# Light experts: float32 weights in two 64-column tiles instead of split weights

## The chip, the cores and the metric

The kernel runs on one core of one Trainium2 chip. The core has five engines that run side by side: TensorE (PE, matrix multiply; its weight loads are listed as PEld), VectorE (DVE), ScalarE (ACT), GpSimd (POOL) and SyncE (SP, which here issues the DMAs). SBUF is the on-chip memory, and PSUM holds what TensorE writes. The metric is the device time of one execution in microseconds (us). Before the change three runs took 1611.48 to 1615.12 us, with a median of 1612.86 us.

## The reference

The program is a trunk of two layers over 256 tokens of width 1024: attention, an output mix, a layer norm, a feed-forward part, a gate and another layer norm. Layer 0 has a dense feed-forward part. Layer 1, which the change touches, has eight experts, of which each token uses two:

```python
gates = jnp.sum(jax.nn.one_hot(top_idx, N_EXPERTS, dtype=jnp.float32) * top_w[..., None], axis=-2)
out = jnp.zeros_like(x)
for e in range(N_EXPERTS):
    out = out + gates[..., e:e + 1].astype(x.dtype) * _swiglu(x, w1[e], w3[e], w2[e])
```

`_swiglu` is `(silu(x @ w1) * (x @ w3)) @ w2`. Of each expert `w1` and `w3` are 1024 x 3584 and `w2` is 3584 x 1024, all float32, so one expert has 44 MB of weights and the eight have 352 MB. Every weight is read once from HBM.

## The kernel before

All matrix products are made in float32r, a format in which TensorE reads a float32 number with reduced precision. To get the precision back, a number is split in two, a rounded `hi` and the rest `lo`: ScalarE casts to `hi` and VectorE subtracts (`Trunk.split`, lines 94 to 96). A product then is three matmuls, hi x hi, hi x lo and lo x hi (`mm3`, lines 251 to 255).

The expert part is the class `Experts` (line 1098 on). Tokens are gathered per expert by a matmul with a one-hot matrix. Experts are ranked by how many tokens chose them. The four that have most, the heavy ones, get 128 token slots each, and the other four, the light ones, 64 each. Tokens that find no slot are served afterwards in a branch that is skipped where there are none.

The weights of an expert are cut along the 3584 hidden columns into blocks of 1024, 1024, 1024 and 512 columns. A block of 1024 is 12 chunks of 1 MB: four of `w1` (kind 0), four of `w3` (kind 1), four of `w2` (kind 2). There are 336 chunks in all, half of them of light experts. The order is fixed when the program is written: two heavy blocks, then light and heavy blocks in turn, with the `w2` chunks of one block laid between the `w1` and `w3` chunks of the next (`parts`, `run`). So a light block's chunks stand beside a heavy block's.

A chunk goes through three places:

- SP issues its DMA into a raw buffer. There are seven, in the order of the list `MOE_RAW` (line 38), and chunk g+7 takes the buffer of chunk g. SP works in order, so a DMA that waits for its buffer holds all later ones.
- ACT and DVE split it into a hi/lo pair of buffers, of which there are four (`MOE_HL`, line 39). After that the raw buffer is free. Splits are written three chunks ahead of the matmuls (`MOE_LEAD`, line 40).
- PE multiplies with the pair. For a heavy expert each 512 columns of one 128-row slice take three matmuls (lines 253 to 255). For a light expert the 64 tokens' hi and lo stand side by side as one 128-column stationary operand: one matmul multiplies both with the weight's hi (line 1232), and a second one the tokens' hi with the weight's lo (line 1233, 64 columns). These are two matmuls in place of three.

A light result thus comes out as two halves in partitions 0 to 63 and 64 to 127, which have to be added. `turn` (line 1278) transposes and adds them at once, by matmuls in plain float32 with the matrix `fold` (line 1288). Then follow Silu on ACT (line 1300) and the product and a new split on DVE (lines 1306 to 1309). A heavy block has Silu and product first and then plain transposes (line 1295). When an expert is done, `close` (line 1336) splits its result, spreads it over the tokens by matmuls (lines 1344 and 1345) and adds it on DVE (line 1349). The last layer norm (lines 651 to 690) ends the program.

Of the kernel before, what the change touches and what calls it, by code (L numbers as in the profile page):

```python
# [19 lines left out]
KT = D // 128  # L20
# [16 lines left out]

MOE_RAW = ["misc", "act", "act", "raw", "raw", "raw", "raw"]
MOE_HL = ["K", "Q", "hl", "hl"]
MOE_LEAD = 3  # L40
HEAVY = 4
# [11 lines left out]
class Trunk:  # L53
# [764 lines left out]
    def route(self, r, N, PL, gate):  # L818
# [60 lines left out]
        r = dict(iota=iota, gate=wt, s1=s1, xs=xs, moe=moe, fold=fold, rank=rank)  # L879
        moe.start(r, PL)  # L880
# [7 lines left out]
        for job in moe.gather(0):  # L888
            job()()
        moe.prepare(4)  # L890
        sums = [lambda tb=tb, j=j: self.ple_sum(PL, [x], t[tb][j], tb, j) for tb in range(2) for j in range(2)]
# [206 lines left out]
class Experts:  # L1098
    def __init__(self, T):
        self.T, self.nc = T, T.nc  # L1100
        self.w = [T.io[n][0] for n in ("moe_w1", "moe_w3", "moe_w2")]
        nb = len(BLOCKS)
        heavy = [(p, b) for p in range(HEAVY) for b in range(nb)]
        light = [(p, b) for p in range(HEAVY, NE) for b in range(nb)]
        self.blocks = [heavy.pop(0), heavy.pop(0)]
        while heavy or light:
            for q in (light, heavy):
                if q:
                    self.blocks.append(q.pop(0))
# [8 lines left out]
        self.raws, self.hl, self.who = [], [], {}  # L1118
        self.jobs, self.pending, self.spread = [], [], {}
        self.hots, self.xe, self.A, self.H, self.Y = {}, {}, {}, {}, {}  # L1120
# [41 lines left out]
    def prepare(self, upto):  # L1162
        T = self.T
        while len(self.hl) < min(upto, len(self.chunks)):
            g = len(self.hl)
            self.fetch(g + 1)
            raw = self.raws[g]
            tag = MOE_HL[g % len(MOE_HL)]
# [21 lines left out]
    def gather(self, g):  # L1190
# [4 lines left out]
        def part(k0):  # L1195
            if k0 == 0:
                self.xe[ps[0]] = T.act([2, KT, CAP], F32R)
                if len(ps) > 1:
                    two = T.act([2, KT, CAP], F32R)
                    for i, p in enumerate(ps[1:]):  # L1200
                        self.xe[p] = two[:, i]
                    self.xe[g, "two"] = two
            hot = self.hots[g]
# [9 lines left out]
            def out():  # L1213
# [3 lines left out]
                if len(ps) > 1:  # L1217
                    two = self.xe[g, "two"]
                    hi, lo = two[:, :, ks, :LIGHT], two[:, :, ks, LIGHT:]
                    src = pt[:, :, CAP:].rearrange("p k (l c) -> p l k c", l=2)  # L1220
                    self.nc.vector.tensor_copy(hi, src)
                    self.nc.vector.tensor_tensor(lo, src, hi.bitcast(F32), op=OP.subtract)

# [3 lines left out]

    def mul(self, out, p, two, hi, lo, first, last):
        mm = self.nc.tensor.matmul
        if not self.light(p):  # L1230
            return self.T.mm3(out, *two, hi, lo, first, last)
        full = lambda: mm(out, two, hi, start=first, stop=last)  # L1232
        half = lambda: mm(out[:LIGHT], two[:, :LIGHT], lo, start=False, stop=False)  # L1233
        for f in (half, full) if last else (full, half):
            f()

    def up(self, i, kind, c, P):
        p, b = self.blocks[i]
        hi, lo = self.hl[self.at[i, kind, c]]
        xe, n = self.xe[p], hi.shape[1]  # L1240
        for k in range(n):
            kk = n * c + k
            two = xe[:, kk, :] if self.light(p) else (xe[:, 0, kk, :], xe[:, 1, kk, :])
            for m, pt in enumerate(P):
                f = slice(512 * m, 512 * (m + 1))
                self.mul(pt, p, two, hi[:, k, f], lo[:, k, f], kk == 0, kk == KT - 1)

    def down(self, i, c):
        p, b = self.blocks[i]
        hi, lo = self.hl[self.at[i, 2, c]]  # L1250
        if b == 0 and c == 0:
            self.Y[p] = [self.T.ps([512], "accB" if self.light(p) else "accA") for _ in range(2)]
        n = self.width(i) // 128
        for k in range(2):
            kk = 2 * c + k
            h = self.H[i][kk // 4]
            two = h[:, kk % 4, :] if self.light(p) else (h[0][:, kk % 4, :], h[1][:, kk % 4, :])
            for m in range(2):
                f = slice(512 * m, 512 * (m + 1))
                self.mul(self.Y[p][m], p, two, hi[:, k, f], lo[:, k, f],  # L1260
                         b == 0 and kk == 0, b == len(BLOCKS) - 1 and kk == n - 1)

    def gated(self, i, kind, P):
        T, nc = self.T, self.nc
        if self.light(self.blocks[i][0]):
            got = [T.s2k([512], tag=("prob", "ckv")[kind]) for _ in P]
            for t, p in zip(got, P):
                nc.scalar.copy(t, p)
            self.A[i, kind] = got
        elif kind == 0:  # L1270
            self.A[i, 0] = [T.s2k([512], tag="prob") for _ in P]
            for t, p in zip(self.A[i, 0], P):
                nc.scalar.activation(t, p, AF.Silu)
        else:
            for t, p in zip(self.A[i, 0], P):
                nc.vector.tensor_tensor(t, t, p, op=OP.mult)

    def turn(self, i):
        T, nc = self.T, self.nc
        self.H[i] = []  # L1280
        todo = []
        cols = lambda t: t.rearrange("m (c p k) -> m c k p", c=2, k=2)
        if self.light(self.blocks[i][0]):
            for a, b in zip(self.A.pop((i, 0)), self.A.pop((i, 1))):
                pt = T.ps([2, 4, LIGHT])
                for n, t in enumerate((a, b)):
                    for k in range(4):
                        nc.tensor.matmul(pt[:, n, k, :], cols(t)[:, k // 2, k % 2, :], self.r["fold"],
                                         start=True, stop=True)
                todo.append((pt, T.shape(a[:, :4 * LIGHT], [4, LIGHT])))  # L1290
        else:
            for s in self.A.pop((i, 0)):
                pt = T.ps([4, 128])
                for k in range(4):
                    nc.tensor.transpose(pt[:, k, :], cols(s)[:, k // 2, k % 2, :], T.ident)
                todo.append((pt, None))

        for pt, s in todo:
            if s is not None:
                nc.scalar.activation(s, pt[:, 0], AF.Silu)  # L1300
        for pt, s in todo:
            if s is None:
                h = T.s2k([4, CAP], F32R, "probT"), T.s2k([4, CAP], F32R, "probT")
                T.split(*h, pt)
            else:
                nc.vector.tensor_tensor(s, s, pt[:, 1], op=OP.mult)
                h = T.s2k([4, CAP], F32R, "probT")
                nc.vector.tensor_copy(h[:, :, :LIGHT], s)
                nc.vector.tensor_tensor(h[:, :, LIGHT:], s, h[:, :, :LIGHT].bitcast(F32), op=OP.subtract)  # L1309
            self.H[i].append(h)  # L1310
# [25 lines left out]
    def close(self, p):  # L1336
        T, r = self.T, self.r
        yy = T.scatter_split(self.Y.pop(p))

        def add(tb, j):  # L1340
            hotT = self.spread[p]["hotT"]
            t = slice(tb * 128, (tb + 1) * 128)
            pt = T.ps([512])
            self.nc.tensor.matmul(pt, hotT[:, t], yy[j][0], start=True, stop=False)
            self.nc.tensor.matmul(pt, hotT[:, t], yy[j][1], start=False, stop=True)

# [28 lines left out]
    def run(self):  # L1375
        T, nc = self.T, self.nc
        n = len(self.blocks)
        for i in range(n + 1):
# [5 lines left out]
            for kind, cs in self.parts(i):  # L1384
                b = i - (kind == 2)
                if kind < 2:
                    P = [T.ps([512]) for _ in range(self.width(i) // 512)]
                for c in cs:
# [164 lines left out]
```

## Time and profile before

| | |
|---|---|
| median of three runs | 1612.86 us |
| the profiled execution, its own time | 1612.92 us |
| its span, first to last instruction | 1611.2 us |
| PE busy | 1559.6 us, 97% of the span |
| PEld busy | 1324.3 us, 82% |
| DVE busy | 1349.8 us, 84% |
| ACT busy | 1093.6 us, 68% |
| HBM read | 467.21 MB |

The profile is of one execution. "Busy" is the time in which at least one instruction of the engine ran. Matmuls overlap each other at their ends, so a matmul's listed duration is longer than the distance from its start to the next one's start. Where this text counts the cost of a stream of matmuls it goes by that distance. A matmul in plain float32 leaves two records in this profile for one instruction of the program (224 instructions of line 1288, 448 records), and one in float32r or a transpose leaves one. The form `128*64 128x512` of a matmul means that 128 rows by 64 columns of weights were loaded and 512 columns were streamed past them. The expert weights arrive between about 641 and 1578 us.

### The profile page before, as it was taken

To read this page: it belongs to the slowest core of one execution; us is meant where nothing else is said; L and a number is where in the kernel's file an instruction comes from. 1 tells how busy PE (TensorE), PEld (TensorE's weight loads), DVE (VectorE), ACT (ScalarE), POOL (GpSimd) and SP (SyncE) were. 2 spreads that over 40 slices of the span, in tenths; PEclk is the share of its full clock that TensorE was granted. 3 is DMA by queue.
4 is the path that set the end of the run, shared out by engine and by line. 5 is a ranking of instruction groups with operands and counts; after the bars stand their busy time and mean duration, and the time that the engine had idled before them with its cause. 6 is when DMAs were issued, how large, how long until landed. Compare 5 with 4: busy or idle time off the path is not lost. (4 is left out here: it accounts for less than half of the span.)

```text
span 1611.2 us, 23371 instructions
## 1 busy us (share of the span) xinstructions
PE 1559.6 (97%) x8969; PEld 1324.3 (82%) x8969; DVE 1349.8 (84%) x1383; ACT 1093.6 (68%) x1185; POOL 66.3 (4%) x113
## 2 busy tenths in 40 slices
PE   8999999999999999989999999999999999999995
PEld 7999989999899999877877876777777777768773
DVE  5797766454668977789999999999999999999997
ACT  4577555444556674667888777768777887787883
POOL 3310000000012001000000000000000000000000
PEclk9999999999999999999999999999999999999998
DMA  8354646555542746669999999999999999999992
GB/s 286 101 167 154 221 161 201 184 188 193 193 144 56 214 162 218 236 224 350 399 407 412 410 407 379 387 355 404 405 389 386 378 394 411 401 379 383 407 407 112
DMA packets 164981, 469.84 MB, mean 292 GB/s; under 512 B 10120, under 2 KB 68560, under 8 KB 150528
## 3 DMA queue, kind: packets, MB, share of 16 engines
q1 hardware_dynamic: 162400, 462.19, 77.1%
q0 software_dynamic: 2176, 5.58, 1.4%
q8 instruction: 72, 1.18, 0.3%
q10 hardware_dynamic: 288, 0.52, 0.1%
q14 instruction: 45, 0.37, 0.1%
HBM read 467.21 MB, written 1.05 MB: 291 GB/s over the span
## 5 line engine op out<-in xcount | busy, mean ns | idle before, releaser
L96 DVE TENSOR_TENSOR hl<-raw,hl 128x1024 fp32r<-128x1024 f32 (+3 forms) x304 | 454.4, 1509 | 129.0 <-ACT hl L95 128.0
L95 ACT CAST hl<-raw 128x1024 fp32r<-128x1024 f32 (+3 forms) x304 | 384.9, 1281 | 200.3 <-PE mm L255 110.7
L255 PE MATMUL mm<-act,hl 128*128 128x256 f32 x1080 | 307.2, 285 | 0.0
L253 PE MATMUL mm<-act,hl 128*128 128x256 f32 x1080 | 307.1, 284 | 0.0
L254 PE MATMUL mm<-act,hl 128*128 128x256 f32 x1080 | 306.5, 284 | 0.0
L253 PEld LDWEIGHTS mm<-act,hl 128*128 128x128 f32 x1080 | 207.9, 192 | 1.3
L254 PEld LDWEIGHTS mm<-act,hl 128*128 128x128 f32 x1080 | 207.7, 192 | 0.8
L255 PEld LDWEIGHTS mm<-act,hl 128*128 128x128 f32 x1080 | 207.7, 192 | 0.4
L96 DVE TENSOR_TENSOR Q<-raw,Q 128x2048 fp32r<-128x2048 f32 (+1 forms) x52 | 114.5, 2205 | 7.6 <-ACT Q L95 7.4
L96 DVE TENSOR_TENSOR K<-raw,K 128x2048 fp32r<-128x2048 f32 (+1 forms) x52 | 114.6, 2205 | 5.4 <-ACT K L95 5.3
L96 DVE TENSOR_TENSOR hl<-act,hl 128x2048 fp32r<-128x2048 f32 x48 | 109.1, 2286 | 2.7 <-ACT hl L95 2.4
L95 ACT CAST Q<-raw 128x2048 fp32r<-128x2048 f32 (+1 forms) x52 | 96.0, 1849 | 20.9 <-PE mm L254 9.6
L1232 PE MATMUL mm<-hl,act 128*128 128x512 f32 x256 | 102.2, 399 | 1.2 <-DVE act L1349 1.2
L95 ACT CAST K<-raw 128x2048 fp32r<-128x2048 f32 (+1 forms) x52 | 95.9, 1847 | 10.9 <-PE mm L254 6.4
L95 ACT CAST hl<-act 128x2048 fp32r<-128x2048 f32 x48 | 91.0, 1914 | 17.4 <-PE mm L254 12.2
L1233 PE MATMUL mm<-hl,act 128*64 128x512 f32 x256 | 98.8, 399 | 0.0
L254 PE MATMUL mm<-hl,act 128*128 128x512 f32 x192 | 75.7, 394 | 2.7 <-DVE hl L96 2.7
L253 PE MATMUL mm<-hl,act 128*128 128x512 f32 x192 | 75.9, 395 | 0.0
L255 PE MATMUL mm<-hl,act 128*128 128x512 f32 x192 | 75.4, 393 | 0.0
L1232 PEld LDWEIGHTS mm<-hl,act 128*128 128x128 f32 x256 | 48.6, 190 | 24.9 <-DVE act L1349 2.6
L1232 PE MATMUL accB<-hl,probT 128*128 128x512 f32 x152 | 60.1, 396 | 2.1 <-DVE probT L1309 2.1
L1233 PE MATMUL accB<-hl,probT 128*64 128x512 f32 x152 | 60.2, 400 | 0.0
(386 smaller groups left out, 3481.0 us busy)
## 6 DMA issues: line engine op xcount, KB each, us to landing
raw<-in_moe_w_dram SPq DMA_DIRECT2D x192, 1024.0 KB, 7.8
act<-in_moe_w_dram SPq DMA_DIRECT2D x96, 1024.0 KB, 10.4
misc<-in_moe_w_dram SPq DMA_DIRECT2D x48, 1024.0 KB, 7.7
raw<-in_w_in_dram SPq DMA_DIRECT2D x35, 1024.0 KB, 5.4
raw<-in_ffn_w_dram SPq DMA_DIRECT2D x33, 1024.0 KB, 5.4
raw<-in_w_out_dram SPq DMA_DIRECT2D x8, 1024.0 KB, 6.0
raw<-in_w_ple_gate_dram SPq DMA_DIRECT2D x8, 1024.0 KB, 5.0
raw<-in_w_uq_dram SPq DMA_DIRECT2D x12, 384.0 KB, 3.3
```

Source lines behind the costliest of these rows:

```text
L95: self.nc.scalar.copy(hi, src)
L96: self.nc.vector.tensor_tensor(lo, src, hi.bitcast(F32), op=OP.subtract)
L253: mm(out, ah, bh, start=first, stop=False)
L254: mm(out, ah, bl, start=False, stop=False)
L255: mm(out, al, bh, start=False, stop=last)
L1232: full = lambda: mm(out, two, hi, start=first, stop=last)
L1233: half = lambda: mm(out[:LIGHT], two[:, :LIGHT], lo, start=False, stop=False)
```

## The change

For the light experts there is no hi/lo split of weights or tokens any more. Their 64 tokens are kept in float32 (`few`), and the raw float32 weights go straight into TensorE as the streamed operand. `side` issues two float32 matmuls with the same 64 token columns: the first takes the left half of the chunk's columns and writes partitions 0 to 63, which is the left 64-column tile of the array, and the second takes the right half and writes partitions 64 to 127, the right tile. One 512-column PSUM tile then holds 1024 result columns, without anything to add up. So `fold` goes, the light blocks take the heavy ones' path of Silu, product and transposes, and `turn` ends in a plain copy. In `close` the two halves are read from the two groups of partitions. A raw buffer of a light chunk is now held until PE is done with it, and a new method `refill` issues further loads after each chunk's matmuls. There are nine raw buffers (two more, from the tag `Q`) and three hi/lo pairs. Splits are written two chunks ahead instead of three. Heavy experts compute as before.

```diff
-MOE_RAW = ["misc", "act", "act", "raw", "raw", "raw", "raw"]
-MOE_HL = ["K", "Q", "hl", "hl"]
-MOE_LEAD = 3
+MOE_RAW = ["misc", "act", "act", "raw", "raw", "raw", "raw", "Q", "Q"]
+MOE_HL = ["K", "hl", "hl"]
+MOE_LEAD = 2
...
-        fold = one([CAP // 2], "fold")
-        nc.vector.tensor_tensor(fold, self.ident[:, :LIGHT], self.ident[:, LIGHT:], op=OP.add)
...
     def prepare(self, upto):
         T = self.T
-        while len(self.hl) < min(upto, len(self.chunks)):
-            g = len(self.hl)
+        while len(self.hl) < len(self.heavy) and self.heavy[len(self.hl)] < upto:
+            g = self.heavy[len(self.hl)]
             self.fetch(g + 1)
             raw = self.raws[g]
...
             T.split(*hl, raw)
-            self.hl.append(hl)
-            self.fetch(g + 1 + len(MOE_RAW))
+            self.hl[g] = hl
+
+    def refill(self, g):
+        while g < len(self.chunks) and (g in self.hl or g in self.used):
+            g += 1
+        self.fetch(g + len(MOE_RAW))
...
-    def mul(self, out, p, two, hi, lo, first, last):
-        mm = self.nc.tensor.matmul
-        if not self.light(p):
-            return self.T.mm3(out, *two, hi, lo, first, last)
-        full = lambda: mm(out, two, hi, start=first, stop=last)
-        half = lambda: mm(out[:LIGHT], two[:, :LIGHT], lo, start=False, stop=False)
-        for f in (half, full) if last else (full, half):
-            f()
+    def side(self, out, lhsT, raw, first, last):
+        n = raw.shape[-1] // 2
+        for m in range(2):
+            self.nc.tensor.matmul(out[m * LIGHT:(m + 1) * LIGHT, :n], lhsT, raw[:, m * n:(m + 1) * n],
+                                  start=first, stop=last)
...
         for k in range(n):
             kk = n * c + k
-            two = xe[:, kk, :] if self.light(p) else (xe[:, 0, kk, :], xe[:, 1, kk, :])
+            if self.light(p):
+                self.side(P[0], xe[:, kk, :], self.raws[g][:, k, :], kk == 0, kk == KT - 1)
+                continue
...
     def turn(self, i):
...
-            for a, b in zip(self.A.pop((i, 0)), self.A.pop((i, 1))):
-                pt = T.ps([2, 4, LIGHT])
-                for n, t in enumerate((a, b)):
-                    for k in range(4):
-                        nc.tensor.matmul(pt[:, n, k, :], cols(t)[:, k // 2, k % 2, :], self.r["fold"],
-                                         start=True, stop=True)
...
+            for k in range(n):
+                nc.tensor.transpose(pt[:, k, :], s[:, k // 2, k % 2, :], T.ident)
+            todo.append((pt, n))
+        for pt, n in todo:
+            if light:
+                h = T.s2k([n, 128], tag="probT")
+                nc.scalar.copy(h, pt)
...
     def close(self, p):
         T, r = self.T, self.r
-        yy = T.scatter_split(self.Y.pop(p))
+        yy = []
+        for y in self.Y.pop(p):
+            yy.append((T.s2k([512], F32R), T.s2k([512], F32R)))
+            T.split(*yy[-1], y)
...
                     else:
                         self.down(b, c)
+                    self.refill(self.at[b, kind, c])
```

What stands in PE's row for the first chunk of the first light block (`act_7748` and `act_7744` are its tokens, `K` the split weights before). Before the change:

```order
L1232 MATMUL mm_7973<-K_7917,act_7748 128x512
L1233 MATMUL mm_7973<-K_7918,act_7748 64x512
L1232 MATMUL mm_7974<-K_7917,act_7748 128x512
L1233 MATMUL mm_7974<-K_7918,act_7748 64x512
L1232 MATMUL mm_7973<-K_7917,act_7748 128x512
L1233 MATMUL mm_7973<-K_7918,act_7748 64x512
L1232 MATMUL mm_7974<-K_7917,act_7748 128x512
L1233 MATMUL mm_7974<-K_7918,act_7748 64x512
L1295 MATMUL mm_7989<-ident,prob_7813 128x128 x4
L1295 MATMUL mm_7994<-ident,prob_7814 128x128 x4
```

And after it, with the three light chunks that follow:

```order
L1230 MATMUL mm_7953<-act_7705,act_7744 64x512 x4
L1289 MATMUL mm_7960<-ident,prob_7807 128x128 x4
L1289 MATMUL mm_7965<-ident,prob_7808 128x128 x4
L1230 MATMUL mm_7953<-raw_7741,act_7744 64x512 x4
L1230 MATMUL mm_7953<-raw_7770,act_7744 64x512 x4
L1230 MATMUL mm_7953<-raw_7802,act_7744 64x512 x4
```

Eight float32r matmuls into two PSUM tiles have become four float32 matmuls into one, left and right tile in turn, and their weights are the raw buffers.

SP's row in the middle of the expert part, with what each DMA waits for. Before:

```order
L169 DMA raw_8577<-in_moe_w_dram 128x2048 [waits DMAHW1_49,DVE_49]
L169 ISA
L169 DMA misc_8591<-in_moe_w_dram 128x2048 [waits DMAHW2_49,DVE_49]
L169 ISA
L169 DMA act_8605<-in_moe_w_dram 128x2x1024
L169 ISA
L169 DMA act_8627<-in_moe_w_dram 128x2x1024 [waits DMAHW3_49,DVE_49]
```

After, at the same place of the queue:

```order
L169 DMA Q_8394<-in_moe_w_dram 128x2048 [waits DMAHW0_49,PE_49]
L169 ISA
L169 DMA misc_8396<-in_moe_w_dram 128x2048 [waits DMAHW1_49,DVE_49]
L169 ISA
L169 DMA act_8398<-in_moe_w_dram 128x2x1024 [waits DMAHW2_49]
L169 ISA
L169 DMA act_8416<-in_moe_w_dram 128x2x1024 [waits DMAHW3_49,DVE_49]
```

Loads that waited for a split on DVE wait for PE now where the buffer's last chunk was a light one, and the buffers `Q` have joined the ring.

## Rows read from the trace of the kernel before

**Rows 1.** Stretches of the run: from:to, length, then the busy time and instruction count of PE, PEld, DVE, ACT and POOL, the granted TensorE clock as a share of full speed, the DMA engines' busy share and the GB/s that they moved. In order: the first expert loads, the body of the expert part, the end of the program, a long dense stretch, and a short one of those with most traffic.

```profile
641.00:735.00 94.00, 87.52 (x433) 71.88 (x432) 78.32 (x131) 58.54 (x74) 1.57 (x2) 0.98 0.68 245
735.00:1578.00 843.00, 823.18 (x3855) 641.55 (x3854) 804.20 (x536) 667.74 (x480) 0.00 (x0) 1.00 1.00 394
...
1578.00:1612.00 34.00, 16.40 (x67) 10.92 (x65) 22.53 (x32) 7.22 (x15) 1.53 (x2) 0.80 0.12 46
...
790.00:900.00 110.00, 108.74 (x508) 83.88 (x507) 105.71 (x68) 91.55 (x66) 0.00 (x0) 1.00 1.02 410
...
1460.00:1470.00 10.00, 10.00 (x59) 8.84 (x59) 8.54 (x9) 5.78 (x5) 0.00 (x0) 1.00 1.03 418
```

**Rows 2.** Who waited for whom from 735 to 1578 us, first of the DMA queue of SP, then of all engines: total us, times, longest us.

```profile
SPq L169 <- DVE hl L96: 291.4, 113, 9.3
SPq L169 <- DVE K L96: 152.2, 53, 9.0
SPq L169 <- DVE Q L96: 148.1, 61, 6.7
...
ACT Q L95 <- PE mm L254: 21.8, 29, 1.4
ACT hl L95 <- PE mm L254: 21.2, 29, 1.5
```

**Rows 3.** Groups of ACT from 735 to 1578 us: the split of one chunk into the pair `K`, with busy us, mean ns and the idle time before them with its causes; the only one of the long groups with a wait for a load.

```profile
L95 ACT CAST K<-raw 128x2048 fp32r<-128x2048 f32 x46 | 88.0, 1913 | 10.0 <-PE mm L254 5.6 <-PE accA L254 2.5 <-DMA raw<-in_moe_w_dram 1.2
```

**Rows 4.** The matmuls of line 1232 over the whole run, by form: count, busy us, mean ns. Line 1233 has the same counts.

```profile
L1232 PE MATMUL mm<-hl,act 128*128 128x512 f32 x256 | 102.2, 399 | 1.2 <-DVE act L1349 1.2
...
L1232 PE MATMUL accB<-hl,probT 128*128 128x512 f32 x152 | 60.1, 396 | 2.1 <-DVE probT L1309 2.1
...
L1232 PE MATMUL mm<-Q,act 128*128 128x512 f32 x96 | 38.7, 403 | 0.0
L1232 PE MATMUL mm<-K,act 128*128 128x512 f32 x96 | 37.6, 391 | 0.0
...
L1232 PE MATMUL accB<-K,probT 128*128 128x512 f32 x36 | 14.2, 393 | 0.9 <-DVE probT L1309 0.9
L1232 PE MATMUL accB<-Q,probT 128*128 128x512 f32 x36 | 14.1, 391 | 0.0
```

**Rows 5.** PE in order of time: start us, us, what. First a piece of a light block, from the first to the ninth of a run of alternating matmuls, then the same of a heavy block.

```profile
1204.99 0.39 PE L1232 MATMUL mm<-Q,act 128*128 128x512 f32 x1
1205.22 0.40 PE L1233 MATMUL mm<-Q,act 128*64 128x512 f32 x1
...
1206.84 0.39 PE L1232 MATMUL mm<-hl,act 128*128 128x512 f32 x1
...
1211.30 0.39 PE L253 MATMUL accA<-K,probT 128*128 128x512 f32 x1
...
1213.12 0.39 PE L255 MATMUL accA<-K,probT 128*128 128x512 f32 x1
```

**Rows 6.** PE in order of time, plain float32: 16 records of 128 columns in the first layer's norm (line 1477) and what follows them, then the 32 fold records of a light block (line 1288), of 64 columns, and what follows.

```profile
221.34 1.95 PE L1477 MATMUL mm<-s2k,act 128*128 128x128 f32 x16
223.04 0.48 PE L253 MATMUL mm<-K,s2k 128*128 128x512 f32 x1
...
1235.13 1.04 PE L1288 MATMUL mm<-fold,prob 128*128 128x64 f32 x8
...
1238.80 0.48 PE L253 MATMUL mm<-Q,act 128*128 128x512 f32 x1
```

**Rows 7.** The fold matmuls over the whole run, by form, and eight transposes of a heavy block in order of time with the matmul after them.

```profile
L1288 PE MATMUL mm<-fold,ckv 128*128 128x64 f32 x224 | 31.0, 281 | 0.0
...
L1288 PE MATMUL mm<-fold,prob 128*128 128x64 f32 x224 | 29.9, 277 | 0.0
...
1203.34 1.34 PE L1295 MATMUL mm<-ident,prob 128*128 128x128 f32 x8 [1.02 <-DVE prob L1276]
1204.44 0.48 PE L1232 MATMUL mm<-Q,act 128*128 128x512 f32 x1
```

**Rows 8.** The largest group of DVE from 735 to 1578 us, one chunk's subtraction each.

```profile
L96 DVE TENSOR_TENSOR hl<-raw,hl 128x2048 fp32r<-128x2048 f32 x90 | 203.6, 2286 | 7.1 <-ACT hl L95 7.1
```

**Rows 9.** Loads of expert weights over the whole run: count, KB each, median us from issue to landing.

```profile
raw<-in_moe_w_dram SPq DMA_DIRECT2D x192, 1024.0 KB, 7.8
act<-in_moe_w_dram SPq DMA_DIRECT2D x96, 1024.0 KB, 10.4
misc<-in_moe_w_dram SPq DMA_DIRECT2D x48, 1024.0 KB, 7.7
```

**Rows 10.** The end of the program in order of time: SP's last issue of expert weights, the split of the last expert's result and its adds on DVE, and the first instruction of the last norm.

```profile
1559.58 6.94 SPq L169 DMA_DIRECT2D raw<-in_moe_w_dram  x4
...
1594.38 1.28 DVE L96 TENSOR_TENSOR s2k<-accB,s2k 128x512 fp32r<-128x512 f32 x2
1595.58 3.38 DVE L1349 SCALAR_TENSOR_TENSOR act<-mm,gate_at,act 128x512 f32<-128x512 f32 x5
1599.10 1.29 DVE L672 BATCH_NORM_STATS2 tiny<-act 128x6 f32<-128x512 f32 x2
```

More of the change, by code (lines that the diff above doesn't have):

```diff
@@ L1117, in __init__ @@
                     self.chunks.append((i - (kind == 2), kind, c))
-        self.raws, self.hl, self.who = [], [], {}
-        self.jobs, self.pending, self.spread = [], [], {}
+        self.raws, self.hl, self.who = [], {}, {}
+        self.heavy = [g for g, (i, kind, c) in enumerate(self.chunks) if not self.light(self.blocks[i][0])]
+        self.jobs, self.pending, self.spread, self.used = [], [], {}, set()
         self.hots, self.xe, self.A, self.H, self.Y = {}, {}, {}, {}, {}
@@ L1197, in part @@
                 self.xe[ps[0]] = T.act([2, KT, CAP], F32R)
[L1198 to L1202, printed above, removed]
+                if g == 1:
+                    self.few = T.act([NE - HEAVY, KT, LIGHT])
+                    for p in range(HEAVY, NE):
+                        self.xe[p] = self.few[:, p - HEAVY]
             hot = self.hots[g]
@@ L1217, in out @@
                 if len(ps) > 1:
[L1218 to L1222, printed above, removed]
+                    self.nc.vector.tensor_copy(self.few[:, ps[1] - HEAVY:ps[2] - HEAVY + 1, ks, :],
+                                               pt[:, :, CAP:].rearrange("p k (l c) -> p l k c", l=2))
@@ L1244, in up @@
             for m, pt in enumerate(P):
                 f = slice(512 * m, 512 * (m + 1))
-                self.mul(pt, p, two, hi[:, k, f], lo[:, k, f], kk == 0, kk == KT - 1)
+                self.T.mm3(pt, xe[:, 0, kk, :], xe[:, 1, kk, :], hi[:, k, f], lo[:, k, f], kk == 0, kk == KT - 1)
+        self.used.add(g)
     def down(self, i, c):
         p, b = self.blocks[i]
-        hi, lo = self.hl[self.at[i, 2, c]]
+        g = self.at[i, 2, c]
         if b == 0 and c == 0:
-            self.Y[p] = [self.T.ps([512], "accB" if self.light(p) else "accA") for _ in range(2)]
+            self.Y[p] = [self.T.ps([512], "accB")] if self.light(p) else [self.T.ps([512], "accA") for _ in range(2)]
@@ L1255, in down @@
             kk = 2 * c + k
+            first, last = b == 0 and kk == 0, b == len(BLOCKS) - 1 and kk == n - 1
+            if self.light(p):
+                h = self.H[i][0]
+                m, at = divmod(kk, n // 2)
+                self.side(self.Y[p][0], h[:, at, m * LIGHT:(m + 1) * LIGHT], self.raws[g][:, k, :], first, last)
+                continue
+            hi, lo = self.hl[g]
             h = self.H[i][kk // 4]
-            two = h[:, kk % 4, :] if self.light(p) else (h[0][:, kk % 4, :], h[1][:, kk % 4, :])
             for m in range(2):
                 f = slice(512 * m, 512 * (m + 1))
-                self.mul(self.Y[p][m], p, two, hi[:, k, f], lo[:, k, f],
-                         b == 0 and kk == 0, b == len(BLOCKS) - 1 and kk == n - 1)
+                self.T.mm3(self.Y[p][m], h[0][:, kk % 4, :], h[1][:, kk % 4, :], hi[:, k, f], lo[:, k, f], first, last)
+        self.used.add(g)
     def gated(self, i, kind, P):
         T, nc = self.T, self.nc
[L1265 to L1272, printed above, removed]
+        if kind == 0:
+            self.A[i] = [T.s2k([p.shape[-1]], tag="prob") for p in P]
+            for t, p in zip(self.A[i], P):
                 nc.scalar.activation(t, p, AF.Silu)
         else:
-            for t, p in zip(self.A[i, 0], P):
+            for t, p in zip(self.A[i], P):
                 nc.vector.tensor_tensor(t, t, p, op=OP.mult)
@@ L1343, in add @@
             pt = T.ps([512])
-            self.nc.tensor.matmul(pt, hotT[:, t], yy[j][0], start=True, stop=False)
-            self.nc.tensor.matmul(pt, hotT[:, t], yy[j][1], start=False, stop=True)
+            rows = slice(LIGHT * j, LIGHT * (j + 1)) if light else slice(0, CAP)
+            for n, y in enumerate(yy[0 if light else j]):
+                self.nc.tensor.matmul(pt, hotT[rows, t], y[rows], start=(n == 0), stop=(n == 1))
             def out():
@@ L1386, in run @@
                 if kind < 2:
-                    P = [T.ps([512]) for _ in range(self.width(i) // 512)]
+                    w = self.width(i)
+                    P = [T.ps([w // 2])] if self.light(self.blocks[i][0]) else [T.ps([512]) for _ in range(w // 512)]
                 for c in cs:
```

39 lines of the change are left out of this document (14 added, 25 removed).

## The prediction

> **What bounds the kernel now.** I read the stretches of the expert part first, because the whole-run shares mix it with layers that the change doesn't touch. From 735 to 1578 us [rows 1] PE is busy 823.18 of 843 us, DVE 804.20 of 843, and the DMA engines show a share of 1.00 at 394 GB/s. Three resources stand near their limit at once, so the question is which one the others wait for. The waits answer it [rows 2]: SP's load queue waited 291.4 + 152.2 + 148.1 = 592 us for splits to give up a raw buffer, and ACT's splits waited for PE to give up a hi/lo pair. Hardly anything waited for a load: one group of ACT shows 1.2 us of it [rows 3]. Weights are there before they are needed, PE eats them up, and everything else is held back by PE. But the reserve behind it is thin: where the loads ran densest for long they moved 410 GB/s (790 to 900 us), and 418 in one of the best 10 us [rows 1], against 394 on average. So a PE that gets much faster runs into the loads after about 4%.
>
> **The light matmuls.** Before, lines 1232 and 1233 ran 256 + 152 + 96 + 96 + 36 + 36 = 672 times each [rows 4], 1344 records of 512 columns. In a light block eight of them start within 1206.84 - 1204.99 = 1.85 us, one each 0.231 us, and in a heavy block within 1213.12 - 1211.30 = 1.82 us, one each 0.2275 us [rows 5]. Light matmuls so cost 1344 x 0.231 = 311 us. Now 608 float32 matmuls of 512 columns and 128 of 256 take their place, as much as 672 of 512. A float32 matmul is two records, so 1344 records of 512 columns again. What remains open is how long one takes, and whether the left and the right tile run at the same time.
>
> The trace has no float32 matmul of 512 columns. The two ends: 0.2275 us, if it streams like the float32r rows; and 0.425 us, if the 128-column float32 records, 16 in 223.04 - 221.34 = 1.70 us, one each 0.106 us [rows 6], are four times as long at four times the columns. They could also be held by their weight loads, since the 64-column fold records are no shorter, 32 in 3.67 us or 0.115 us each [rows 6]; that is why both ends stay open. I take 0.425 us, from the row that is float32 itself. The Trainium skill ("FP8 and Floating Point Precision", TensorE Precision Notes) counts four passes through the array for true float32; with two records that makes two passes each, the upper end, and the sum by it is the same 0.425 us.
>
> No row of before has two column tiles at work at once. Here too there are two ends: one after the other, 1344 x 0.425 = 571 us, or fully side by side, half of it, 286 us. I take side by side: the two matmuls share no array column and no result partition, and each reads its own half of the chunk. That makes 286 - 311 = -25 us. The other corners are 571 - 311 = +260 us (0.425, in turn), 306 - 311 = -5 us (0.2275, in turn) and 153 - 311 = -158 us (0.2275, side by side).
>
> Changing between the whole array and a half of it costs little in this trace: line 1232 loads 128 columns and line 1233 only 64, they alternate, and the step is 0.231 us against 0.2275 us without alternation [rows 5]. The program now goes between light matmuls and others 150 times. I go by the row and count 150 x 0.004 = 0.6 us as nothing. The Trainium skill ("TensorEngine Tiling (Array Packing)", Key Properties) says that a change of the tiling mode drains TensorE, which speaks against such a program. By that rule each change would cost the part of a matmul that the next one overlaps, 0.39 - 0.23 = 0.16 us [rows 5], together 24 us, which the loads' limit below would cover; the 1344 matmuls that alternate here show no such cost.
>
> **Folds, transposes, splits.** The 224 + 224 fold records [rows 7] at 0.115 us go: -51 us. For them 56 plain transposes come (four for a 1024 block, two for a 512 block, for four experts), at (1204.44 - 1203.34) / 8 = 0.1375 us [rows 7]: +8 us. Half of the 336 chunk splits go, 168 x 2.286 = 384 us of DVE [rows 8] and 168 x 1.913 = 321 us of ACT [rows 3]. All of that lies beside PE, so in the sum it counts nothing; it takes DVE from 95% of the stretch to about half. Where a heavy block's transposes wait for DVE now, 1.02 us once [rows 7], a light block has the same wait in place of the fold's chain of ACT and DVE; I count these even. PE's sum is -25 - 51 + 8 = -68 us.
>
> **What is late next.** PE can give back 68 us only if the weights come 68 us sooner. In 843 us at 394 GB/s 332 MB were moved. At 410 GB/s they take 810 us, 33 us less; at 418, 795 us, 48 us less; without any gain in rate, 0. I take 410, the rate of a long stretch. So the loads are late, not PE, and 33 of the 68 us come out. Before 735 us nothing is won: the first 24 chunks are heavy, and PE eats one in 12 x 0.2275 = 2.73 us. Two more raw buffers let 2 MB more be asked for there, between 0 and 5 us at 410 GB/s; I take 0.
>
> At the end PE now follows the loads instead of trailing them. Loads end at about 1578 us (the last is issued at 1566 [rows 10]) and the last norm starts at 1599.10 us, 21 us later. What must stand there: the last chunk's 1.7 us, the split of one result tile instead of two, 0.6 + 0.7 us, and four adds of 0.7 us with their matmuls, together about 7 us. So 0 to 14 us can go; I take half, 7.
>
> **The new waits.** A light matmul waits for its load itself, and the load into a buffer that held a light chunk waits for PE. Behind that waiting load stand all later loads, since SP works in order. Chunk g+9 is asked for when PE is done with g, or two or more chunks sooner after a heavy g. A chunk every 2.56 us (1.05 MB at 410 GB/s) makes nine chunks 23 us, against 7.8 to 10.4 us from issue to landing [rows 9]. So I charge nothing. A heavy split takes 1.9 + 2.3 = 4.2 us, and two light chunks ahead of it last only 3.4 us, but ACT and DVE are free to start when the load lands, and a fixed delay moves all chunks alike; it costs nothing while the loads set the pace.
>
> **Sum.** The profiled execution took 1612.92 us, within 0.1 us of the median, so it needs no correction. 1612.9 - 33 - 7 = 1573 us.
>
> **Rivals.**
>
> 1. The tiles run one after the other. The matmuls are issued in one order on one engine, and nothing in the trace shows two at once. Then PE has +260 - 51 + 8 = +217 us, and as it bounds already, the time is 1830 us. It decides from the gain s of the pairing: PE has 571 / s - 311 - 43, which is a loss below s = 1.61. Against it stands only that the two tiles need nothing of each other.
> 2. They overlap in part, because each float32 matmul is two records that must follow each other in its tile, and the second tile's first record queues behind them. With s from 1.45 to 1.75 PE has +40 to -28 us, and the time is 1585 to 1653 us; in the middle, at 1.60, 357 - 354 = +3 us and 1616 us, no faster than before. The Trainium skill ("TensorE: Matmul & The Clock Gate", Part 3, Measured speedup vs the span model) has 2.38 times for three column tiles, 79% of three; two tiles at 79% would give that 1.59, so 1618 us. No row here shows it.
> 3. The loads don't get faster: they run at 394 GB/s because the DMA engines are as full as they get (a share of 1.00 on average), and buffers held longer eat up the rest. Then only the end gains, 1606 us. For it: the share; against it: 410 GB/s over 110 us.
> 4. A float32 record streams at 0.2275 us. PE gains 48 or 201 us and the loads still bound, so this gives the forecast's 1573 us and is counted with it.
>
> **How the numbers follow.** The forecast with rival 4 gets 0.70; its own range is 1550 us (418 GB/s and all 14 us of the end) to 1600 us (a pairing of 1.8, with small losses between loads and PE). Rival 1 gets 0.13, rival 2 0.12, rival 3 0.05. The range of 1550 to 1640 us takes in the forecast's, rival 3 and most of rival 2, and leaves out rival 1 and what lies beyond the ends, about 0.2. What can be told from no change is 0.2%, about 3 us. Faster is the forecast, 0.70, with rival 3's larger part and a piece of rival 2, 0.75 together; the same is 0.04; slower is rival 1 and most of rival 2, 0.21.
>
> **What would show it.** Right: in a light block the start of the right tile's record lies inside the left tile's, and a chunk's four float32 matmuls (eight records) take about 1.7 us; the DMA rate from 780 us on stands near 410 GB/s throughout; PE shows idle time before light matmuls, released by loads; DVE falls to about half. Wrong: eight records take 3.4 us and PE is busy throughout (rival 1), or 2.1 us and more (rival 2); SP still waits long, now for PE, while the rate stays under 400 GB/s (rival 3). A light record of about 0.23 us would show the upper end of its price wrong without touching the time.

## The result and the profile after

The changed kernel takes 1573.39 us (median of four, 1571.93 to 1575.25) against 1612.34 us of the kernel before. The ratio is 0.9756, with a 95% interval of 0.9739 to 0.9773. The forecast was 1573 us.

The stretches after, in the columns of [rows 1]. The body of the expert part ends earlier now, so it is taken to 1545 us, and the last two rows cover the end of the loads:

```profile
641.00:735.00 94.00, 88.90 (x448) 72.78 (x447) 77.64 (x130) 58.81 (x75) 1.57 (x2) 1.00 0.73 267
735.00:1545.00 810.00, 788.14 (x3601) 486.20 (x3602) 425.97 (x294) 340.89 (x261) 0.00 (x0) 0.99 1.02 406
735.00:780.00 45.00, 45.00 (x206) 29.53 (x206) 27.25 (x19) 21.12 (x16) 0.00 (x0) 1.00 0.89 335
780.00:900.00 120.00, 115.66 (x507) 68.54 (x505) 58.29 (x36) 50.50 (x40) 0.00 (x0) 0.99 1.02 410
900.00:1000.00 100.00, 100.00 (x473) 66.81 (x472) 63.78 (x43) 46.55 (x34) 0.00 (x0) 1.00 1.02 411
...
1530.00:1540.00 10.00, 10.00 (x71) 5.32 (x71) 1.77 (x4) 2.14 (x4) 0.00 (x0) 1.00 1.04 409
1540.00:1550.00 10.00, 9.46 (x53) 3.84 (x50) 1.17 (x2) 0.74 (x2) 0.00 (x0) 1.00 0.72 294
```

From 780 us on the loads move 410 or 411 GB/s in stretch after stretch, where they moved 394 on average before. DVE is busy 426 of 810 us, about half. The loads run dry at about 1547 us (294 GB/s over the last 10 us, against 409 in the 10 before). In the kernel before, 373 GB/s from 1570 to 1580 us put that end at 1579 us by the same reckoning, 32 us later. Of before, in the same columns, the first stretch after 735 us and the two at the end of the loads:

```profile
735.00:780.00 45.00, 45.00 (x210) 35.75 (x209) 43.02 (x31) 36.61 (x26) 0.00 (x0) 1.00 0.95 359
1560.00:1570.00 10.00, 9.87 (x59) 7.98 (x57) 9.96 (x8) 7.98 (x9) 0.00 (x0) 1.00 1.03 401
1570.00:1580.00 10.00, 9.23 (x40) 6.36 (x41) 9.90 (x11) 9.84 (x8) 0.00 (x0) 1.00 0.91 373
```

The last norm (line 672) now starts 12 us behind the loads, where it was 20 us behind them [rows 10]:

```profile
1559.50 1.29 DVE L672 BATCH_NORM_STATS2 tiny<-act 128x6 f32<-128x512 f32 x2 [1.76 <-DVEq L1013]
```

PE's matmuls at the border of a heavy and a light piece: start us, us, what. Then the weight loads of the same light matmuls:

```profile
806.71 0.39 PE L255 MATMUL mm<-hl,act 128*128 128x512 f32 x1
807.03 1.94 PE L1230 MATMUL accB<-raw,probT 128*64 128x512 f32 x8
808.79 1.89 PE L1230 MATMUL accB<-Q,probT 128*64 128x512 f32 x8
```

```profile
807.94 0.14 PEld L1230 LDWEIGHTS accB<-raw,probT 128*64 128x64 f32 x2 [0.28 <-issue]
808.37 0.14 PEld L1230 LDWEIGHTS accB<-Q,probT 128*64 128x64 f32 x2 [0.28 <-issue]
808.80 0.14 PEld L1230 LDWEIGHTS accB<-Q,probT 128*64 128x64 f32 x2 [0.29 <-issue]
```

A chunk's eight records start within 808.79 - 807.03 = 1.76 us, 0.22 us each. By itself that fits two stories: records of 0.43 us side by side, or records of 0.22 us in turn, as in [rows 5]. The weight loads speak for the first: they come two at a time (x2 in one merged row of 0.14 us, the length of a single one), and the next two 0.43 us later. So two records start together and stream for 0.43 us; the one-tile kernel below tests this.

The waits after, from 735 to 1545 us, in the form of [rows 2]: first those of SP, then two of all engines, and last the loads' time from issue to landing, as in [rows 9]:

```profile
SPq L169 <- PE mm L1230: 148.1, 69, 8.6
SPq L169 <- PE accB L1230: 134.2, 39, 6.4
SPq L169 <- DVE hl L96: 70.5, 39, 5.8
```

```profile
ACT hl L95 <- DMA raw<-in_moe_w_dram: 77.8, 27, 10.3
...
ACT hl L95 <- DMA act<-in_moe_w_dram: 46.5, 12, 10.3
```

```profile
raw<-in_moe_w_dram SPq DMA_DIRECT2D x148, 1024.0 KB, 15.9
```

Before, ACT waited for PE and hardly ever for a load. Now it waits for loads, and a load needs 15.9 us from issue to landing instead of 7.8. By an estimate from these figures, 15.9 us at 406 GB/s make 6.5 MB, some six chunks on their way at once, where 7.8 us at 394 GB/s made three. SP's waits for PE are still long, but they cost nothing while the rate stays at 411 GB/s.

### The profile page after: what moved, and what is told of

Read it like the earlier page. It is cut to its first block, busy times and chain, and to the rows that moved or that the text cites. A ratio compares the mean times of both kernels' runs of the same rounds, so it can differ in the third digit from the quotient of the medians.

```text
span 1571.6 us, 22033 instructions
## 1 busy us (share of the span) xinstructions
PE 1519.3 (97%) x8705; PEld 1162.5 (74%) x8705; DVE 961.8 (61%) x1134; ACT 763.4 (49%) x961; POOL 66.3 (4%) x113
## 5 line engine op out<-in xcount | busy, mean ns | idle before, releaser
L96 DVE TENSOR_TENSOR hl<-raw,hl 128x1024 fp32r<-128x1024 f32 (+3 forms) x264 | 365.4, 1392 | 213.4 <-ACT hl L95 205.2
L95 ACT CAST hl<-raw 128x1024 fp32r<-128x1024 f32 (+3 forms) x264 | 309.8, 1183 | 274.7 <-PE mm L255 111.2
L254 PE MATMUL accA<-hl,probT 128*128 128x512 f32 x172 | 72.3, 420 | 16.6 <-DVE hl L96 16.5
L1230 PE MATMUL mm<-raw,act 128*64 128x512 f32 (+1 forms) x440 | 87.1, 537 | 0.0
L253 PE MATMUL accA<-hl,probT 128*128 128x512 f32 x172 | 73.3, 426 | 4.7 <-ACT hl L95 4.7
L96 DVE TENSOR_TENSOR hl<-act,hl 128x2048 fp32r<-128x2048 f32 x22 | 50.3, 2291 | 43.8 <-ACT hl L95 43.8
L255 PE MATMUL accA<-hl,probT 128*128 128x512 f32 x172 | 70.5, 410 | 0.0
L95 ACT CAST hl<-act 128x2048 fp32r<-128x2048 f32 x22 | 42.0, 1907 | 57.4 <-DMA act<-in_moe_w_dram 46.5
L254 PE MATMUL mm<-K,act 128*128 128x512 f32 x172 | 67.4, 392 | 0.7 <-DVE K L96 0.7
L253 PE MATMUL mm<-K,act 128*128 128x512 f32 x172 | 67.5, 392 | 0.0
L255 PE MATMUL mm<-K,act 128*128 128x512 f32 x172 | 67.2, 391 | 0.0
L95 ACT CAST probT<-mm 128x512 fp32r<-128x512 f32 x28 | 15.2, 588 | 106.0 <-PE mm L1289 106.0
L253 PEld LDWEIGHTS mm<-hl,act 128*128 128x128 f32 x276 | 52.0, 188 | 18.9 <-issue 4.9
## 6 DMA issues: line engine op xcount, KB each, us to landing
raw<-in_moe_w_dram SPq DMA_DIRECT2D x148, 1024.0 KB, 15.9
```

Source lines behind the costliest of these rows:

```text
L95: self.nc.scalar.copy(hi, src)
L253: mm(out, ah, bh, start=first, stop=False)
L254: mm(out, ah, bl, start=False, stop=False)
L255: mm(out, al, bh, start=False, stop=last)
L1230: self.nc.tensor.matmul(out[m * LIGHT:(m + 1) * LIGHT, :n], lhsT, raw[:, m * n:(m + 1) * n], start=first, stop=last)
```

## The experiments

**Is it the pairing, and what does it hang on?** Two kernels leave bytes, instructions and records as they are. The first only sorts a light chunk's matmuls (shown for `up`; `down` has the same edit, and `side` gets the tile `t` as an argument):

```diff
-        for k in range(n):
+        for t, k in [(t, k) for t in range(2 if self.light(p) else 1) for k in range(n)]:
...
```

> Only the order of a light chunk's matmuls changes: all of the left tile first, then all of the right tile; the work and the result are the same. Theory (a float32 record of 512 columns takes 0.43 us, matmuls start in order, a tile takes one at a time, and the two tiles run side by side): a tile's four records now follow each other, and only the last of one tile lies beside the first of the other, so a chunk takes 6 steps of 0.43 us instead of 4. 152 chunks x 0.86 us and 16 chunks of the 512 blocks x 1.29 us are +152 us of PE, less the 35 us that PE had to spare: 1690 us, eight records in 2.58 us instead of 1.72. Rival (a record takes 0.22 us and they run one after the other, nothing is side by side): no change, 1573 us. Rival (PE looks past the order): no change either.

Measured: 1574.4 us, ratio 0.9755 (0.9735 to 0.9774), no change. Its weight loads from 807.4 us on:

```profile
807.99 0.15 PEld L1229 LDWEIGHTS accB<-raw,probT 128*64 128x64 f32 x2 [0.28 <-issue]
808.42 0.15 PEld L1229 LDWEIGHTS accB<-raw,probT 128*64 128x64 f32 x2 [0.28 <-issue]
```

They still come in twos every 0.43 us. In a chunk of a 1024 block the right tile's first record now stands four records behind the left tile's first, and the two tiles fill all the same. So the theory's in-order part is wrong there. The time alone doesn't say that the order never matters, since PE has some 37 us to spare (worked out below). In a `w1` or `w3` chunk of a 512 block eight records of 256 columns go to one tile and then eight to the other, and there the order does cost something. Sixteen such records, first in the changed kernel and then in this one:

```profile
915.68 1.90 PE L1230 MATMUL mm<-raw,act 128*64 128x256 f32 x16
915.78 2.81 PE L1229 MATMUL mm<-raw,act 128*64 128x256 f32 x16
```

The 0.91 us more are about four steps of the 0.22 us that such a record takes alone in the next kernel. This fits a right tile that starts four records ahead of its place and no more: behind four left records nothing is lost, and behind eight the first four of the left and the last four of the right run alone. What takes the records out of the program's order, PE itself or a step before it, these runs don't show.

The second kernel puts nearly all matmuls into the left tile. The right half of the result is left out so, and its products are added to the left half:

```diff
         for m in range(2):
-            self.nc.tensor.matmul(out[m * LIGHT:(m + 1) * LIGHT, :n], lhsT, raw[:, m * n:(m + 1) * n],
-                                  start=first, stop=last)
+            t = m if first else 0
+            self.nc.tensor.matmul(out[t * LIGHT:(t + 1) * LIGHT, :n], lhsT, raw[:, m * n:(m + 1) * n],
+                                  start=first, stop=(last and m == 1) or t == 1)
```

> The second of each two light matmuls goes to the left tile too, apart from the first of each sum, which still writes both; the right half of the result is left out and added to the left half. Records, bytes and instructions are as many as before. Theory (side by side): 304 of 336 pairs lose their overlap, 0.86 us each: +261 us of PE, less 35 us to spare: 1799 us, eight records in 3.4 us. Rival (records of 0.22 us one after the other): no change, 1573 us.

Measured: 1798.57 us, ratio 1.1144 (1.1119 to 1.1168). Its matmuls and weight loads in one light piece:

```profile
820.12 3.65 PE L1231 MATMUL accB<-raw,probT 128*64 128x512 f32 x8
823.60 0.59 PE L1231 MATMUL accB<-Q,probT 128*64 128x512 f32 x1
```

```profile
820.60 0.14 PEld L1231 LDWEIGHTS accB<-raw,probT 128*64 128x64 f32 x1 [0.29 <-issue]
821.03 0.14 PEld L1231 LDWEIGHTS accB<-raw,probT 128*64 128x64 f32 x1 [0.29 <-issue]
```

Eight records start within 823.60 - 820.12 = 3.48 us, twice as long, and the weight loads come singly every 0.43 us. Records that stream in less time, with a fixed cost for two in a row in one tile, would look the same at 512 columns. The records of 256 columns rule that out. The busy time of both forms over the whole run of this kernel:

```profile
L1231 PE MATMUL mm<-raw,act 128*64 128x512 f32 x312 | 132.9, 596 | 0.0
...
L1231 PE MATMUL mm<-raw,act 128*64 128x256 f32 x128 | 28.8, 383 | 0.0
```

132.9 / 312 = 0.426 us and 28.8 / 128 = 0.225 us for one: about half for half of the columns. A float32 record of 512 columns so takes 0.43 us, and without the second tile the change would have cost about 185 us.

**Who sets the pace now?** One kernel takes work from PE, one takes bytes from the loads, and one has both edits:

```diff
+        w = n if first or last else n // 2
         for m in range(2):
-            self.nc.tensor.matmul(out[m * LIGHT:(m + 1) * LIGHT, :n], lhsT, raw[:, m * n:(m + 1) * n],
+            self.nc.tensor.matmul(out[m * LIGHT:(m + 1) * LIGHT, :w], lhsT, raw[:, m * n:m * n + w],
```

> Light matmuls other than the first and the last of each sum stream only half of their columns; the other half of these products is left out. Loads are as before. PE loses 272 x 0.43 = 117 us. Theory (the loads set the pace): 1570 to 1573 us, and the rate stays at 411 GB/s. Rival (PE still sets it): 1456 to 1500 us.

```diff
+            if self.light(self.blocks[i][0]) and kind < 2:
+                src, dims = src[:, :dims[0] // 2, :], [dims[0] // 2, dims[1]]
...
```

> Of each light w1 and w3 chunk only the first half is loaded, and it is multiplied twice; the other half of these weights is left out. PE's work is as before, and the loads are 112 x 0.52 = 59 MB fewer, 143 us at 411 GB/s. Theory (the loads set the pace, with PE 35 us behind): PE sets it now, 1530 to 1550 us. Rival (something else than the loads sets the pace): 1573 us. Rival (loads alone, PE far from the limit): 1430 us.

> Both cuts together: half of the light w1 and w3 weights is not loaded (the other half is multiplied in its place), and light matmuls stream half of their columns but for the first and the last of each sum. Theory (two limits, loads first and PE 35 us behind): PE has 117 us less and the loads 143 us less, so 1430 to 1460 us, well under either cut alone. Rival (a third limit, as the heavy splits or the chain of Silu, product and transposes): about the 1530 to 1550 us of the loads' cut alone.

Measured: 1570.04 us with less for PE (ratio 0.9725, 0.9709 to 0.9742), 1536.78 us with fewer loads (0.9522, 0.9506 to 0.9538), 1445.87 us with both (0.896, 0.8934 to 0.8987). The dense stretch of the changed kernel, then of the first of these, in the columns of [rows 1]:

```profile
780.00:1545.00 765.00, 743.14 (x3397) 456.68 (x3397) 398.72 (x275) 319.77 (x246) 0.00 (x0) 0.99 1.02 410
780.00:1545.00 765.00, 670.89 (x3391) 468.72 (x3389) 395.39 (x274) 316.79 (x244) 0.00 (x0) 0.93 1.02 410
```

And of the second:

```profile
780.00:1510.00 730.00, 730.00 (x3399) 450.27 (x3398) 395.23 (x275) 317.39 (x245) 0.00 (x0) 1.00 0.93 356
```

With less work PE stands idle for 94 of 765 us, the loads stay at 410 GB/s, and the time hardly moves. Its busy time falls by 72 us and not by the 117 us of the expectation, because the granted clock averages 0.93 of full speed there instead of 0.99: at full speed it would be 743.14 x 0.99 - 670.89 x 0.93 = 112 us, an estimate. With fewer loads PE is busy all the time, and the rate falls to 356 GB/s. So the loads set the pace of the changed kernel, with PE close behind: 1573.39 - 1536.78 = 37 us. With both cuts the time falls as far as the theory of two limits has it, so no third one stands near them.

**The buffers.** First seven raw buffers,

```diff
-MOE_RAW = ["misc", "act", "act", "raw", "raw", "raw", "raw", "Q", "Q"]
+MOE_RAW = ["misc", "act", "act", "raw", "raw", "raw", "raw"]
```

> Seven raw buffers instead of nine, all else as in the changed kernel. Theory (nine buffers are more than the loads need): seven chunks of 2.56 us are 18 us, against 8 to 10 us from issue to landing without a queue, so 1573 to 1580 us. Rival (a buffer held until PE is done needs the depth): 1590 us or more, with the load rate under 400 GB/s.

and then also the pairs and the distance of before:

```diff
-MOE_HL = ["K", "hl", "hl"]
-MOE_LEAD = 2
+MOE_HL = ["K", "Q", "hl", "hl"]
+MOE_LEAD = 3
```

> Seven raw buffers, four hi/lo pairs and splits three chunks ahead, as before the change, with the new light matmuls. Theory (the gain is the matmuls', not the buffers'): 1573 to 1580 us, as with seven buffers alone. Rival (the buffers bring the gain): 1590 us or more.

Measured: 1577.36 us, ratio 0.9766 (0.9745 to 0.9786), and 1580.93 us, ratio 0.9797 (0.9771 to 0.9823). The first can't be told from the changed kernel's 0.9756, the second lies some 0.4% above it. So two raw buffers fewer cost at most a few us, though PE holds those of light chunks longer now.

**Was freeing DVE and ACT worth nothing?** The prediction had said so. This kernel splits the light chunks again, and nothing reads their pairs:

```diff
...
-        while len(self.hl) < len(self.heavy) and self.heavy[len(self.hl)] < upto:
-            g = self.heavy[len(self.hl)]
+        while self.split_to < min(upto, len(self.chunks)):
+            g = self.split_to
+            self.split_to += 1
...
             T.split(*hl, raw)
-            self.hl[g] = hl
+            if not self.light(self.blocks[self.chunks[g][0]][0]):
+                self.hl[g] = hl
```

> ACT and DVE split the light chunks too, into the three pairs in turn, and nobody uses the result; the light matmuls read the raw buffers as in the changed kernel. That puts 168 x 2.29 = 384 us of DVE and 322 us of ACT back. Theory (splits lie beside the work that sets the pace): DVE has 783 us to do in a body of 810 us, so 1573 to 1590 us. Rival (freeing DVE is what made the kernel faster): back to 1605 us or more.

Measured: 1609.77 us, ratio 0.9982 (0.9972 to 0.9992). The rival's time came: nearly all of the gain is gone. Whether its reason holds, DVE alone, is tested below. The stretch from 735 to 1545 us, and PE's two longest waits from 735 to 1578 us:

```profile
735.00:1545.00 810.00, 769.14 (x3461) 474.87 (x3459) 751.04 (x443) 617.13 (x409) 0.00 (x0) 0.99 1.00 393
```

```profile
PE accA L254 <- DVE K L96: 21.4, 13, 4.1
PE accA L254 <- DVE hl L96: 16.3, 11, 2.4
```

The loads are back at 393 GB/s, and PE waits 38 us for heavy splits. ACT in turn waits for PE to release a pair. From 735 to 1545 us the two longest of these waits, which with two shorter ones make 150 us, are

```profile
ACT K L95 <- PE accA L254: 49.8, 21, 4.9
ACT hl L95 <- PE mm L254: 44.1, 54, 1.8
```

Three more kernels put the idle splits into the pair `Q` of their own, with seven raw buffers: both halves of a split, DVE's half alone and ACT's half alone. In the kernel with both halves the added lines are

```diff
+            if self.light(self.blocks[self.chunks[g][0]][0]):
+                self.fetch(g + 1)
+                raw = self.raws[g]
+                hi, lo = [T.act(list(raw.shape[1:]), F32R, tag="Q") for _ in range(2)]
+                T.split(hi, lo, raw)
+                continue
```

and the other two have `T.nc.vector.tensor_tensor(lo, raw, raw, op=OP.subtract)` or `T.nc.scalar.copy(hi, raw)` in the place of `T.split(hi, lo, raw)`.

> The idle splits of light chunks again, but into a pair of their own (the buffers Q), so that the heavy chunks keep their three pairs for themselves; seven raw buffers, so to be compared with the 1577 us of that kernel. Theory A (the idle splits cost 36 us because they took the pairs that heavy splits needed): 1577 to 1585 us. Theory B (they cost it because ACT and DVE were occupied, DVE for 782 of 843 us, and heavy splits stood in line behind them): 1600 us or more.

> Only DVE's half of the idle splits, in the same place: a subtraction of one chunk into the pair Q, with nothing on ACT. Theory B with DVE as the engine that matters: nearly all of the loss, 1598 us or more. With the chain from ACT to DVE as the cause (each subtraction waits for its cast): less than half of it, under 1590 us.

> Only ACT's half of the idle splits: a cast of one chunk into the pair Q, with nothing more on DVE. ACT has about 640 of 843 us to do then. Theory B with DVE as the engine that matters: 1577 to 1585 us. If ACT's place in line matters as much: 1590 us or more.

Measured: 1791.64 us (ratio 1.1101, 1.1081 to 1.1121), 1581.88 us (0.9811, 0.9791 to 0.9831) and 1583.15 us (0.9815, 0.9795 to 0.9834). The first is no answer to its question, since the single pair became a bottleneck of its own. ACT in that kernel:

```profile
1017.43 1.91 ACT L95 CAST Q<-raw 128x2048 fp32r<-128x2048 f32 x1 [2.75 <-DVE Q L96]
1021.71 1.90 ACT L95 CAST Q<-misc 128x2048 fp32r<-128x2048 f32 x1 [2.36 <-DVE Q L96]
```

The next cast waits until the subtraction has released the pair, so a light split takes 4.28 us. Heavy splits come late behind it: from 735 to 1545 us PE waits 42.9 us for their casts and 41.5 us for their subtractions. The other two are clear. DVE's half alone brings DVE to 771 of 810 us:

```profile
735.00:1545.00 810.00, 782.95 (x3570) 479.87 (x3568) 771.28 (x456) 339.62 (x258) 0.00 (x0) 0.99 1.01 405
```

and yet the time is only about 5 us over the 1577 us of seven buffers. ACT's half alone costs about 6. So the occupation of one engine doesn't explain 36 us, and the two halves added make 11. What remains is what only both together have: the chain from cast to subtraction, and the pairs that it holds. The last kernel has the idle splits of the first of these four in the ring of pairs, with the three settings of before (seven raw buffers, four pairs, three chunks of distance) from the two diffs on buffers:

> The idle splits of light chunks in the ring of four hi/lo pairs, with seven raw buffers and splits written three chunks ahead: the buffers of the kernel before and its splits, with the new light matmuls. To be compared with 1581 us of the same buffers without idle splits. Theory A (three pairs were too few for all chunks: a split chain of 4.2 us waits for a pair that PE still reads): 1581 to 1592 us. Theory B (ACT and DVE together have too little room for 336 splits, however many pairs): 1600 us or more.

Measured: 1596.95 us, ratio 0.991 (0.9887 to 0.9932), between the two theories. ACT's longest wait of its splits for loads, and PE's two longest waits:

```profile
ACT hl L95 <- DMA raw<-in_moe_w_dram: 27.6, 43, 1.7
```

```profile
PE mm L1291 <- DVE prob L1279: 14.0, 12, 2.4
PE accA L254 <- DVE K L96: 7.4, 7, 1.3
```

With four pairs in place of three, two raw buffers fewer and one chunk more of distance, idle splits cost 16 us (against the 1581 us of the same buffers) instead of 36. ACT's waits for PE to release a pair are 74 us in place of 150, which points to the pairs as what the other 20 us hung on; no run changes the pairs alone. The 16 us are not far from the 11 us that the two halves cost by themselves. PE waits 14.0 us for the product on DVE, where splits are busy too (766 of 810 us). How the 16 us divide between that wait, the pairs and the loads was not taken apart further.

These runs make a ladder. From the kernel before to the new matmuls with old buffers and idle splits: ratio 0.991, about 15 us. Without the splits: 0.9797, about 18 us more by the ratios and 16 by the medians. With the new buffers: 0.9756, about 7 us more. What a rung is worth depends on the order: with the new buffers and the idle splits only some 3 us of the gain are there (0.9982).

## Why the prediction was right, and where it was not

- *The bound before.* That PE bounds and the loads are close behind holds, but it is not the whole list. The sum for PE, -68 us and -7 us at the end, gives 1538 us where the loads are out of the way, and the kernel with half of the light loads took 1536.78 us. The splits stood nearer than the loads: with them put back on the old buffers the kernel takes 1597 us, some 15 us under before, where the loads allow 1573 us.
- *The price of the float32 record.* 0.425 us was taken, 0.43 us was measured. The lower end of the bounds, 0.2275 us, is refuted by the one-tile kernel. The four passes that the Trainium skill counts ("FP8 and Floating Point Precision", TensorE Precision Notes) fit: two records, each 0.43 / 0.2275 = 1.9 times as long as a float32r record.
- *Side by side.* Shown by the one-tile kernel. Rival 1 has its price nearly right (1830 us, where the one-tile kernel took 1798.57 us), but the tiles don't run in turn. Of rival 2 nothing is left in the changed kernel: eight records start within 1.76 us in two tiles and within 3.48 us in one, so the pairing is 1.98.
- *What is late next.* Right, and this made the number: the loads end 32 us sooner (33 forecast), at 410 or 411 GB/s (410 forecast). The last norm moved another 8 us closer to them (7 forecast); that was half of a range of 0 to 14 us, taken without a row that decides it, so there is luck in this hit. The two extra raw buffers did bring 267 against 245 GB/s from 641 to 735 us, but 335 against 359 from 735 to 780, so together little, as forecast.
- *The step that failed: splits.* "All of that lies beside PE, so in the sum it counts nothing." With idle splits put back the kernel takes 1597 us with four pairs and 1610 us with three. Of the gain of 39 us, about 15 us come from the multiplication and the folds as long as splits stay, 16 to 18 us from splits that are gone, and some 7 us from buffers, taken in this order. The sum came out because the loads cap it at the same place whatever frees it: PE alone had 68 us to give, and the loads let 33 of them through. What was not seen is that PE can give them only if the heavy splits keep pace with it. The row of DVE's 804 of 843 us [rows 1] was read and then dropped, because DVE was not what PE waited for before.
- *A sign that didn't show.* PE was to stand idle before light matmuls, released by loads. From 735 to 1545 us it doesn't: the wait shows at ACT, whose heavy splits wait for loads, and PE's longest wait in total is 16.5 us, for heavy splits:

```profile
PE accA L254 <- DVE hl L96: 16.5, 11, 1.8
```

- *Changes between whole and half array.* From the last heavy matmul to the first light one it is 807.03 - 806.71 = 0.32 us instead of 0.2275, so about 0.09 us for a change. The single records of the trace show the same on the way back, 0.52 us to the next heavy matmul instead of 0.43. For 150 changes that is about 14 us of PE, and not the 0.6 us of the prediction. The row taken there, 128 columns in turn with 64, shows 0.004 us a step and so doesn't price this change. The Trainium skill ("TensorEngine Tiling (Array Packing)", Key Properties) says that a change of the tiling mode drains TensorE. The trace agrees that a change costs something, 0.09 us, less than the 0.16 us that the prediction worked out for this rule. PE's slack of 37 us covers it.

## What to carry to other kernels

Where three resources stand near their limit, work out each one's own time after the change, and take the largest as the floor: here the loads at 410 GB/s, read from the densest long stretch of the old trace, gave the end of the loads within a microsecond. But a resource that nobody waits for now is free only as long as the others don't speed up; before counting its relief as nothing, ask whether the faster version could still be fed by it. To learn whether two streams overlap on TensorE, look at the starts of the weight loads, not at the mean distance of the records, and take the second stream away once to see what the first costs alone.

## What the runs showed of the hardware that was not expected

Two things. The two column tiles fill evenly whether the program alternates between them or names four records for one and then four for the other (weight loads in twos every 0.43 us in both). With eight for one and then eight for the other they don't: sixteen records took 2.81 us instead of 1.90. Alternating is the order that loses nothing. And DVE at 771 of 810 us cost 5 us, and ACT at 641 of 810 us 6 us, while both halves of the same work in a chain cost 16 us with four pairs of buffers and 36 us with three: the share of busy time of either engine doesn't show that.
